# Packed 16-bit keys, shared write-back and a longer taper of loads in a NaN-ignoring row maximum

## The chip, the cores and the metric

The kernel runs on one core of one Trainium2 chip. The metric is the device time in microseconds (us) of one execution; a second number, the span, is the profiled time from the first to the last instruction and is about 1.8 us shorter. PE is not used. In the profile ACT is ScalarE, POOL is GpSimd, DVE is VectorE and SPq is the queue that issues the transfers.

## The reference

The input is 32 x 2048 rows of 2048 float32 values, a tenth of them NaN. The output is one maximum per row, NaNs ignored:

```python
def reference(x, axis):
    return np.nanmax(x, axis=axis).astype(np.float32)
```

That is 65,536 rows of 8 KB, 537 MB, read once. Rows are spread over 128 partitions, 512 for each partition. Below, "a row" is one row of every partition: 2048 elements in each partition, 1 MB in all.

## The kernel before

A tile of up to 8 rows is loaded. ScalarE maps the upper 16 bits of every float, as an integer, to a key that puts NaN at the bottom; GpSimd maps the key back; VectorE then takes the float maximum. Both passes touch every second 16-bit element *in place*, in the loaded tile. A last pair of small VectorE operations (`none`, `fin`) marks rows without a number, and a small store follows.

```python
FULL = [[3, 3, 2]]                       # one load of 8 rows, worked on in pieces of 3, 3, 2
GROUPS = [[FULL] * 5] * 12 + [           # 12 groups of five tiles, then four groups of one
    [FULL],
    [[[2, 2], [2], [2]]],                # loads of 4, 2, 2
    [[[2], [2], [1], [1], [1], [1]]],
    [[[1], [1], [1], [1], [1], [1], [1], [1]]],
]
WIDE = 8
# ... cut ...
io = ctx.enter_context(tc.tile_pool(name="io", bufs=3))      # three tiles of 64 KB a partition
for s, g in zip(rows, GROUPS):
    # ... cut ...
    for tl in g:
        xt = io.tile([P, WIDE * D], i32, tag="xt")
        base = at
        for ld in tl:
            c = sum(ld)
            nc.sync.dma_start(out=xt[...], in_=xg[...])               # L86
            if len(stores) > 1:
                nc.sync.dma_start(**stores.pop(0))                    # L91, same queue
            for c in ld:
                xp = xt[:, (at - base) * D : (at - base + c) * D]
                nc.scalar.activation(                                 # L94
                    out=xp.bitcast(u16)[:, 1::2], in_=xp.bitcast(i16)[:, 1::2],
                    func=PRELU, bias=top, scale=-1.0, alpha=...)
                nc.gpsimd.tensor_scalar(                              # L102
                    out=xp.bitcast(i16)[:, 1::2], in0=xp.bitcast(u16)[:, 1::2],
                    scalar1=-1.0, scalar2=float(TOP), op0=ALU.mult, op1=ALU.add)
                nc.vector.tensor_reduce(out=acc[:, at : at + c], ...) # L110
                at += c
    none = res.tile([P, s], i32, tag="none")
    nc.vector.tensor_scalar(out=none, in0=acc, ...)                   # L118
    fin = res.tile([P, s], i32, tag="fin")
    nc.vector.tensor_tensor(out=fin, in0=acc.bitcast(i32), in1=none, ...)  # L127
    stores.append(dict(out=og, in_=fin))
```

## Time and profile before

| | before |
|---|---|
| time, median | 1284.1 us |
| span | 1282.3 us |
| last input packet ends | 1268.0 us |
| busy: ScalarE, GpSimd, VectorE | 1203, 1204, 1143 us |

Throughput of the input over the run, in 40 equal slices of 32 us (from the page of the profile):

```profile
GB/s 425 425 425 446 438 425 426 442 440 428 425 438 442 429 425 432 448 429 426 429 448 432 425 429 446 433 423 428 448 430 430 427 448 428 431 427 433 304 245 197
```

The input flows at some 433 GB/s until the last three slices, where it drops to 304, 245 and 197. The same in stretches, with how busy each engine was (columns: stretch, its length, busy us and instructions of DVE, ACT and POOL, a clock of no use here, DMA share, GB/s):

```profile
30.00:1180.00 1150.00, 1044.72 (x199) 1112.41 (x178) 1114.15 (x178) 1.00 1.00 433
1180.00:1200.00 20.00, 18.68 (x4) 19.41 (x5) 19.42 (x4) 1.00 0.62 266
1200.00:1220.00 20.00, 19.54 (x6) 20.00 (x5) 19.68 (x5) 1.00 0.92 381
1220.00:1240.00 20.00, 20.00 (x7) 16.32 (x5) 19.68 (x5) 1.00 0.47 187
1240.00:1260.00 20.00, 20.00 (x9) 15.19 (x7) 16.87 (x8) 1.00 0.78 318
1260.00:1285.00 25.00, 19.73 (x12) 11.08 (x5) 13.49 (x6) 1.00 0.32 132
```

Until 1180 us the DMA share is 1.00: the transfers bound the kernel, and ScalarE and GpSimd are just able to follow. Afterwards the DMA has holes, but VectorE and GpSimd are nearly gapless (from 1200 us on, VectorE's longest gap is 0.43 us and GpSimd's 2.65). What each piece of work costs, from the groups by shape (busy us and mean ns of one stand after the bar):

```profile
L94 ACT ACTIVATE xt<-xt,top 128x4096 uint16<-128x4096 int16 x67 | 323.3, 4839 | 0.0
L102 POOL TENSOR_SCALAR xt<-xt 128x4096 int16<-128x4096 uint16 x67 | 318.0, 4746 | 5.3
...
L94 ACT ACTIVATE xt<-xt,top 128x2048 uint16<-128x2048 int16 x12 | 30.0, 2566 | 8.5 <-DMA xt<-in_x_dram 8.5
...
L118 DVE TENSOR_SCALAR none<-acc 128x40 int32<-128x40 f32 x12 | 16.4, 1363 | 0.4
L118 DVE TENSOR_SCALAR none<-acc 128x8 int32<-128x8 f32 x4 | 8.1, 2014 | 0.0
```

Two rows cost ScalarE 4.84 us and one row 2.57, so a further row costs 2.27 us. The DMA brings a row in 2.42. `none`, on 8 to 40 elements, takes 1.4 to 2 us, which can't be work. VectorE's order of time at the end (start, duration):

```profile
1222.33 4.10 DVE L118 TENSOR_SCALAR none<-acc 128x8 int32<-128x8 f32 x1
1226.27 4.41 DVE L110 TENSOR_REDUCE acc<-xt 128x2 f32<-128x4096 f32 x1
1230.60 0.56 DVE L127 TENSOR_TENSOR fin<-acc,none 128x8 int32<-128x8 int32 x1
1231.09 13.06 DVE L110 TENSOR_REDUCE acc<-xt 128x2 f32<-128x4096 f32 x3
1244.07 1.88 DVE L118 TENSOR_SCALAR none<-acc 128x8 int32<-128x8 f32 x1
...
1266.15 13.24 DVE L110 TENSOR_REDUCE acc<-xt 128x1 f32<-128x2048 f32 x6
1279.42 0.17 DVE L118 TENSOR_SCALAR none<-acc 128x8 int32<-128x8 f32 x1
```

The last `none`, when GpSimd has finished, takes 0.17 us; the ones before it, 1.88 to 4.10. In the trace every one of the fifteen before the last ended 0.02 to 0.04 us after the end of a GpSimd instruction that was already running when it started: it waits for GpSimd.

### The profile page before, as it was taken

Reading aid. Unit: us, or ns where it says so; the run is one execution under the profiler, and the core shown is the slowest. Engines: PE = TensorE matmul, PEld = TensorE weight load, DVE = VectorE, ACT = ScalarE, POOL = GpSimd, SP = SyncE. Lnnn points to the kernel's source line nnn. Section 1 sums busy time; section 2 is a strip of 40 time slices with the busy share of each in tenths; the row PEclk is TensorE's granted clock in tenths of the full one; section 3 lists DMA queues with packets and bytes.
Section 4 is the critical chain, followed back from the end, with each engine's and each line's share of the span. In section 5 each row is a group of like instructions: output and inputs, shape, how many; then the busy total and the mean of one; then the engine's idle time right before and its main releaser. Section 6 shows DMA issues by size and latency. Waiting matters only on the chain.

```text
span 1282.3 us, 1065 instructions
## 1 busy us (share of the span) xinstructions
DVE 1142.7 (89%) x234; ACT 1203.3 (94%) x203; POOL 1203.8 (94%) x205
## 2 busy tenths in 40 slices
DVE  0789989989998998998998998998998998998999
ACT  3999999999999999999999999999999999999985
POOL 0999999999999999999999999999999999999996
DMA  9999999999999999999999999999999999999754
GB/s 425 425 425 446 438 425 426 442 440 428 425 438 442 429 425 432 448 429 426 429 448 432 425 429 446 433 423 428 448 430 430 427 448 428 431 427 433 304 245 197
DMA packets 13543, 537.20 MB, mean 419 GB/s; under 512 B 3552, under 2 KB 3552, under 8 KB 3552
## 3 DMA queue, kind: packets, MB, share of 16 engines
q1 hardware_dynamic: 13536, 537.14, 97.1%
q14 instruction: 7, 0.06, 0.0%
HBM read 536.87 MB, written 0.26 MB: 419 GB/s over the span
## 4 chain that ended last, share of the span: by engine, by line
DMA 42%; POOL 23%; DVE 18%; ACT 12%; issue 5%; ACTq 0%; DVEq 0%
DMA xt<-in_x_dram 42%; POOL xt L102 23%; DVE acc L110 18%; ACT xt L94 12%; DVE none L118 1%; DVE fin L127 0%; ACTq L94 0%; DVEq L110 0%; DVEq L127 0%
## 5 line engine op out<-in xcount | busy, mean ns | idle before, releaser
L102 POOL TENSOR_SCALAR xt<-xt 128x6144 int16<-128x6144 uint16 (+2 forms) x201 | 1203.6, 5988 | 69.9 <-ACT xt L94 58.9
L94 ACT ACTIVATE xt<-xt,top 128x6144 uint16<-128x6144 int16 (+2 forms) x201 | 1201.8, 6082 | 67.0 <-DMA xt<-in_x_dram 67.0
L110 DVE TENSOR_REDUCE acc<-xt 128x3 f32<-128x6144 f32 (+2 forms) x201 | 1116.0, 5582 | 135.4 <-POOL xt L102 135.4
L118 DVE TENSOR_SCALAR none<-acc 128x40 int32<-128x40 f32 (+1 forms) x16 | 24.4, 1526 | 0.5
L127 DVE TENSOR_TENSOR fin<-acc,none 128x40 int32<-128x40 int32 (+1 forms) x16 | 4.4, 275 | 0.4
L71 ACT ACT_TABLE_LOAD x1 | 1.3, 1283 | 0.7 <-PEq L149 0.7
L69 DVE MEMSET top<- 128x1 f32 x1 | 0.1, 59 | 0.8 <-PEq L149 0.8
L149 POOL MEMSET const-float32-0.0<- 128x1 f32 x1 | 0.1, 98 | 0.2 <-issue 0.2
L71 ACT ACTIVATE warm<-top 128x1 f32<-128x1 f32 x1 | 0.2, 203 | 0.0
L149 POOL MEMSET const-bfloat16-1.0<- 128x1 bf16 x1 | 0.1, 102 | 0.0
L149 POOL MEMSET const-uint8-127<- 128x1 uint8 x1 | 0.1, 102 | 0.0
L149 POOL MEMSET const-float32-1.0<- 128x1 f32 x1 | 0.1, 98 | 0.0
## 6 DMA issues: line engine op xcount, KB each, us to landing
xt<-in_x_dram SPq DMA_DIRECT2D x12, 1024.0 KB, 9.7
xt<-in_x_dram SPq DMA_DIRECT2D x4, 2048.0 KB, 13.9
xt<-in_x_dram SPq DMA_DIRECT2D x1, 4096.0 KB, 16.1
xt<-in_x_dram SPq DMA_DIRECT2D x61, 25.8
out_dram<-fin SPq DMA_DIRECT2D x12, 20.0 KB, 25.5
out_dram<-fin SPq DMA_DIRECT2D x4, 4.0 KB, 1.4
```

What stands on the lines that cost most here:

```text
L69: nc.vector.memset(top, EDGE)
L71: nc.scalar.activation(out=warm, in_=top, func=PRELU, alpha=0.5)
L94: nc.scalar.activation(out=xp.bitcast(u16)[:, 1::2], in_=xp.bitcast(i16)[:, 1::2], func=PRELU, bias=top, scale=-1.0, alpha=float(TOP - LOW ...
L102: nc.gpsimd.tensor_scalar(out=xp.bitcast(i16)[:, 1::2], in0=xp.bitcast(u16)[:, 1::2], scalar1=-1.0, scalar2=float(TOP), op0=ALU.mult, op1= ...
L110: nc.vector.tensor_reduce(out=acc[:, at : at + c], in_=xp.bitcast(f32).rearrange("p (c d) -> p c d", c=c), axis=mybir.AxisListType.X, op=A ...
L118: nc.vector.tensor_scalar(out=none, in0=acc, scalar1=NONE, scalar2=float(0x00C00000), op0=ALU.is_equal, op1=ALU.mult,)
L127: nc.vector.tensor_tensor(out=fin, in0=acc.bitcast(i32), in1=none, op=ALU.bitwise_or)
L149: nc = _bacc.Bacc("TRN2", target_bir_lowering=False, num_devices=1)
```

## The change

The intent: ScalarE writes its keys packed into small buffers, which should be faster than every second element in place. The time won on ScalarE is spent on writing back one row of seven (negative numbers in the lists), which relieves GpSimd. With some slack on all three engines a long taper of loads and pieces at the end can bring their lag behind the DMA down. Loads have 7 rows, so that three tiles of 56 KB and the key buffers fit. `none` moves to PSUM, and a group is now six tiles, so fewer results come near the end.

```diff
-FULL = [[3, 3, 2]]
-GROUPS = [[FULL] * 5] * 12 + [ ... cut ... ]
-WIDE = 8
+TILES = (                                    # (loads, pieces, reduces)
+    [([1], [1], [1])]
+    + [([7], [1, 2, 2, -1, 1], [1, 2, 2, 2])] * 59
+    + [([7], [2, 2, 1, 2], [4, 1, 2])]
+    + [([7], [1, 2, 2, -2], [3, 2, 2])]
+    ... cut: two more of one load, then [2, 5] and [4, 3] ...
+    + [([4, 3], [2, 2, 2, -1], [2, 2, 3])] * 3
+    + [([1, 3, 3], [1, 1, 1, 1, 2, -1], [1, 2, 1, 3])]
+    + [([3, 2, 2], [1, 1, 1, 1, 1, 1, 1], [2, 1, 1, 1, 1, 1])]
+    + [([2, 1, 2, 1, 1], [1, 1, -1, 1, 1, 1, 1], [3, 2, 1, 1])]
+    + [([1, 1, 1, 1, 1, 1, 1], [1, 1, -1, 1, 1, 1, 1], [3, 1, 1, 1, 1])]
+    + [([1, 1, 1, 1, 1, 1, 1], [1, 1, -1, 1, 1, 1, -1], [1, 2, 1, 1, 1, 1])]
+)
+GROUPS = [TILES[:7]] + [TILES[i : i + 6] for i in range(7, 73, 6)] + [TILES[73:]]
+WIDE = 7
+PIECE = 2
@@
+    mid = ctx.enter_context(tc.tile_pool(name="mid", bufs=4))
+    flag = ctx.enter_context(
+        tc.tile_pool(name="flag", bufs=2, space=bass.MemoryType.PSUM)
+    )
@@ ... cut: loads of a tile first, then one store if due ...
+            for c in pieces:
+                back, c = c < 0, abs(c)
+                xp = xt[:, at * D : (at + c) * D]
+                kt = mid.tile([P, PIECE * D], u16, tag="kt")
+                nc.scalar.activation(                             # L116
+                    out=kt[:, : c * D],
+                    in_=xp.bitcast(i16)[:, 1::2],
+                    func=ACT.Prelu, bias=top, scale=-1.0, alpha=...)
+                if back:
                     nc.scalar.activation(                         # L125
-                        out=xp.bitcast(u16)[:, 1::2],
-                        in_=xp.bitcast(i16)[:, 1::2],
-                        func=PRELU, ...
+                        out=xp.bitcast(i16)[:, 1::2],
+                        in_=kt[:, : c * D],
+                        func=ACT.Copy, bias=float(TOP), scale=-1.0)
+                else:
                     nc.gpsimd.tensor_scalar(                      # L133
                         out=xp.bitcast(i16)[:, 1::2],
-                        in0=xp.bitcast(u16)[:, 1::2],
+                        in0=kt[:, : c * D], ...)
+                at += c
+                while reds and done + reds[0] <= at:
+                    ... cut: tensor_reduce of the next reds[0] rows, L144 ...
-        none = res.tile([P, s], i32, tag="none")
+        none = flag.tile([P, s], i32, tag="none")
```

## The prediction

> **What bounds the kernel now.** From 30 to 1180 us the input DMA bounds it: the windows view gives a DMA share of 1.00 and 433 GB/s, and each 8-row tile starts on ScalarE 19.36 us after the last, having waited about 0.6 us for DMA. But ScalarE, GpSimd and VectorE are at 1112, 1114 and 1045 us busy of those 1150, so none can catch up. At the end the DMA falls to 266, 280, 315 and 348 GB/s from 1180 us on. The queue's timeline shows why: loads wait for VectorE to free a buffer, and result stores stand in the same queue ahead of them. From 1186 us on compute bounds: 32 rows need 94 us from their first activation to the last reduce. At 433 GB/s the whole input needs 1239 us; the span is 1282.
>
> **Costs read from the trace (groups by form).** Per row (from the differences of 1, 2 and 3 rows): ScalarE 2.27 us, GpSimd 2.28, VectorE's reduce 2.14, DMA 2.42; fixed 0.1 to 0.3 us each. The small "none" operation takes 1.4 to 4.1 us while GpSimd runs but 0.17 us at the end when it does not; the Trainium skill ("SBUF — State Buffer", Who interferes with whom) names a port pair that VectorE's two-port modes and GpSimd lock against each other, which agrees.
>
> **What the change does.**
> 1. ScalarE reads the strided keys and writes them packed. The Trainium skill ("ScalarE: Activation LUTs", What ACT_TABLE_LOAD costs) states about 280 ns + 0.833 ns per element; this trace shows 294 + 1.109. I take the strided 16-bit write in place to be what costs the difference, so a packed write should run near 0.84: 1.7 us a row.
> 2. Of 7 rows GpSimd writes back 6 and ScalarE 1, both strided, at about 2.28 a row. Per 7-row tile (DMA 16.94 us), estimated: ScalarE 7 x 1.71 + 2.27 + fixed = 15.6, GpSimd 14.6, VectorE 15.4. Each gets 1.3 us or more of slack per tile.
> 3. "none" goes to PSUM: 12 x 1.2 us off VectorE.
> 4. The end: loads of 7, 4, 3, 2 and finally 1 row over 14 tiles, and stores that no longer block loads. VectorE's lag (28 us) shrinks by 1.3 us a tile, to about 11.
>
> The steady stage stays DMA-bound. All gain is in the last 100 us.
>
> **Sum.** Start 3.2 us, 512 rows at 2.42 = 1239, about 2 for small packets (8 KB packets took 309 ns, 64 KB 2420): last landing near 1244. Then ScalarE twice, reduce, finish: VectorE ends near 1254.5, plus 2.5 for the store and end (as now) = 1257 span, and 1.7 from span to time, as now: **1258 us, 2.0% less, 8 in 10 between 1251 and 1267.** Chances: faster by over 2% 0.52, within 2% 0.40, slower 0.08.
>
> **What would show it.** ScalarE's two-row packed pass at 3.6 to 3.8 us (4.84 now); its one-row write-back at 2.3 to 2.5; GpSimd 4.7 to 4.8 for two rows; "none" below 0.3 us; DMA share near 1.00 until about 1240; the last reduce ending 9 to 12 us after the last landing.
>
> **What would make it wrong.** If the slow ScalarE rate comes from the strided read, ScalarE needs 19.4 us a tile of 16.9 and the time is about 1430. If GpSimd also speeds up on packed input, VectorE gets its data earlier and 2 us come off. If ScalarE's rate is only 0.88 to 0.9, or VectorE has gaps in the taper, 2 to 8 us come on.

## The result, and the profile after

| | before | after |
|---|---|---|
| time, median | 1284.11 us | 1262.16 us |
| ratio, 95% interval | | 0.9829 (0.9812 to 0.9846) |
| span | 1282.3 us | 1260.4 us |
| last input packet ends | 1268.0 us | 1247.8 us |
| busy: ScalarE, GpSimd, VectorE | 1203, 1204, 1143 us | 1124, 1063, 1127 us |

Ratios here are the mean time of one kernel's fast runs over that of the other's of the same rounds, so not quite the ratio of the medians. The gain is 22 us, 1.7%: a clear gain, but under the 2% line.

Throughput of the changed kernel in 40 slices:

```profile
GB/s 412 437 437 437 435 433 417 434 437 437 436 435 435 427 424 437 436 435 437 435 434 424 426 437 435 437 437 433 435 416 437 437 436 437 417 433 430 425 422 211
```

The same stretches as before:

```profile
30.00:1180.00 1150.00, 1046.69 (x288) 1042.67 (x401) 989.50 (x271) 1.00 1.00 433
1180.00:1200.00 20.00, 20.00 (x6) 19.54 (x10) 18.46 (x7) 1.00 1.00 425
1200.00:1220.00 20.00, 17.88 (x7) 19.58 (x10) 19.36 (x9) 1.00 1.01 420
1220.00:1240.00 20.00, 19.93 (x8) 17.73 (x9) 19.03 (x9) 1.00 1.01 420
1240.00:1260.00 20.00, 17.96 (x11) 12.91 (x7) 9.67 (x4) 1.00 0.24 97
```

In the first 1150 us nothing changed for the time: 433 GB/s and a DMA share of 1.00 in both kernels. ScalarE lost 70 us of work there and GpSimd 125, and that time is idle. The whole gain is at the end, where the DMA now stays full until it has nothing more to bring (e6 below shows that a full DMA alone is not the gain). The idle time of ScalarE before each steady tile shows the slack. Here is a tile of 8 rows before and one of 7 rows after (start, duration, the first passes of the tile together; in brackets the idle time before it and what ended it):

```profile
332.93 18.77 ACT L94 ACTIVATE xt<-xt,top 128x6144 uint16<-128x6144 int16 x3 [0.64 <-DMA xt<-in_x_dram]
497.99 12.99 ACT L116 ACTIVATE kt<-xt,top 128x2048 uint16<-128x2048 int16 x5 [1.58 <-DMA xt<-in_x_dram]
```

ScalarE's slack went from 0.6 to 1.6 us a tile and GpSimd's from about 0.5 to 2.5. VectorE had 1.9 us in a tile of 8 rows and has 1.6 in one of 7, no more than before for a row. The groups that answer to those of before:

```profile
L133 POOL TENSOR_SCALAR xt<-kt 128x4096 int16<-128x4096 uint16 x142 | 676.9, 4767 | 79.5 <-ACT kt L116 73.3
L116 ACT ACTIVATE kt<-xt,top 128x4096 uint16<-128x4096 int16 x144 | 525.2, 3694 | 8.5 <-DMA xt<-in_x_dram 8.5
L116 ACT ACTIVATE kt<-xt,top 128x2048 uint16<-128x2048 int16 x224 | 438.2, 1991 | 119.9 <-DMA xt<-in_x_dram 119.9
...
L125 ACT ACTIVATE xt<-kt 128x2048 int16<-128x2048 uint16 x68 | 168.3, 2475 | 0.2
...
L155 DVE TENSOR_SCALAR none<-acc 128x42 int32<-128x42 f32 x11 | 2.3, 205 | 0.4
```

ScalarE's two-row pass went from 4.84 to 3.69 us, GpSimd's hardly changed (4.75 and 4.77), and `none` is down to 0.2 us. A row more costs ScalarE 3.694 - 1.991 = 1.70 us when it writes packed. VectorE's order of time at the end:

```profile
1211.27 30.66 DVE L144 TENSOR_REDUCE acc<-xt 128x3 f32<-128x6144 f32 x9 [2.12 <-POOL xt L133]
1241.96 0.20 DVE L155 TENSOR_SCALAR none<-acc 128x42 int32<-128x42 f32 x1
1242.20 0.20 DVE L164 TENSOR_TENSOR fin<-acc,none 128x42 int32<-128x42 int32 x1
1242.32 15.38 DVE L144 TENSOR_REDUCE acc<-xt 128x1 f32<-128x2048 f32 x6
1257.73 0.17 DVE L155 TENSOR_SCALAR none<-acc 128x7 int32<-128x7 f32 x1
```

VectorE has no gap from 1211 us on and its last reduce ends at 1257.7 us, 9.9 us after the last packet. Before, 11.4 us lay between (1268.0 and 1279.4), but there the last packet itself was late.

### The profile page after: what moved, and what is told of

Its sections match the earlier page's. It is cut to its first block, busy times and chain, and to the rows that moved or that the text cites. A ratio compares the mean times of both kernels' runs of the same rounds, so it can differ in the third digit from the quotient of the medians.

```text
span 1260.4 us, 1707 instructions
## 1 busy us (share of the span) xinstructions
DVE 1127.1 (89%) x319; ACT 1123.5 (89%) x440; POOL 1063.1 (84%) x302
## 4 chain that ended last, share of the span: by engine, by line
DMA 52%; POOL 15%; ACT 13%; DVE 10%; issue 9%; SPq 0%; ACTq 0%; DVEq 0%
DMA xt<-in_x_dram 52%; POOL xt L133 15%; ACT kt L116 12%; DVE acc L144 10%; ACT xt L125 1%; SPq L103 0%; DVE none L155 0%; ACTq L116 0%; DVEq L144 0%; DVE fin L164 0%; ACTq L125 0%
## 5 line engine op out<-in xcount | busy, mean ns | idle before, releaser
L144 DVE TENSOR_REDUCE acc<-xt 128x2 f32<-128x4096 f32 (+2 forms) x292 | 1122.9, 3889 | 129.3 <-POOL xt L133 129.2
L133 POOL TENSOR_SCALAR xt<-kt 128x2048 int16<-128x2048 uint16 (+1 forms) x298 | 1062.9, 3567 | 189.1 <-ACT kt L116 175.7
L116 ACT ACTIVATE kt<-xt,top 128x2048 uint16<-128x2048 int16 (+1 forms) x368 | 951.1, 2657 | 128.4 <-DMA xt<-in_x_dram 128.4
L125 ACT ACTIVATE xt<-kt 128x2048 int16<-128x2048 uint16 x70 | 177.8, 2540 | 0.3
L155 DVE TENSOR_SCALAR none<-acc 128x42 int32<-128x42 f32 (+2 forms) x13 | 2.6, 202 | 0.5
L164 DVE TENSOR_TENSOR fin<-acc,none 128x42 int32<-128x42 int32 (+2 forms) x13 | 2.6, 197 | 0.4
```

What stands on the lines that cost most here:

```text
L116: nc.scalar.activation(out=kt[:, : c * D], in_=xp.bitcast(i16)[:, 1::2], func=ACT.Prelu, bias=top, scale=-1.0, alpha=float(TOP - LOW) / (E ...
L125: nc.scalar.activation(out=xp.bitcast(i16)[:, 1::2], in_=kt[:, : c * D], func=ACT.Copy, bias=float(TOP), scale=-1.0,)
L133: nc.gpsimd.tensor_scalar(out=xp.bitcast(i16)[:, 1::2], in0=kt[:, : c * D], scalar1=-1.0, scalar2=float(TOP), op0=ALU.mult, op1=ALU.add,)
L144: nc.vector.tensor_reduce(out=acc[:, base + done : base + done + n], in_=xt[:, done * D : (done + n) * D] .bitcast(f32) .rearrange("p (c d ...
L155: nc.vector.tensor_scalar(out=none, in0=acc, scalar1=NONE, scalar2=float(0x00C00000), op0=ALU.is_equal, op1=ALU.mult,)
```

## The experiments

My theory: the 22 us come from two things that need each other, slack on the engines (packed keys and shared write-back) and a long taper that uses the slack to make up lag. Rivals: the taper alone; the small things alone (`none` blocked by GpSimd, stores in the load queue); the split of loads alone. Estimates in the expectations come from a recurrence worked by hand from the trace: each piece starts when its data, its engine and its buffer are there, with the durations above.

### The changed kernel with one part undone

**e1: no split loads.**

```diff
+TILES = TILES[:1] + [([7], pieces, reds) for _, pieces, reds in TILES[1:]]
```

> The changed kernel with every load of the taper made one 7-row load; pieces and reduces stay. My theory (the taper lets the engines start on part of a tile, at a small price in DMA time): the last landing comes 2 to 4 us earlier than 1247.8 us (no small packets), but VectorE ends about 10 us later; time 1270 to 1275 (estimate 1272.7). Rival (the split of the loads is worth nothing, the slack of the engines is all): 1258 to 1263, earlier by the saved packets.

Measured: 1274.5 us, ratio to before 0.9925. The last packet ended at 1246.0 us, 1.8 us earlier than in the changed kernel (expected 2 to 4, so a little less), and VectorE's last reduce at about 1269.9, 12 us later. Splitting the loads is worth 12 us and costs 2 us of transfer; the rival falls.

**e2: GpSimd writes back everything.**

```diff
+TILES = [(loads, [abs(c) for c in pieces], reds) for loads, pieces, reds in TILES]
```

> The changed kernel with GpSimd writing back all pieces, none on ScalarE. My theory (GpSimd at 2.29 us a row plus 0.23 a piece needs 17.2 us for a 7-row tile that the DMA brings in 17.0, so it falls behind and no lag is ever made up): 1280 to 1292 (estimate 1287), no better than before, GpSimd gapless. Rival (the taper alone gives the gain): 1262 to 1266.

Measured: 1299.7 us, ratio 1.012: slower than the kernel before, and beyond my range. The direction is the theory's, the size is not. Its first stretch shows why (columns as above):

```profile
30.00:1180.00 1150.00, 1024.71 (x282) 872.02 (x329) 1124.17 (x327) 1.00 1.00 426
```

GpSimd, at 98% of that stretch, holds the DMA down to 426 GB/s. The last packet ended at 1266.4 us, 19 us later than in the changed kernel, and VectorE's last reduce another 29 us later instead of 10. So of the 37 us about half are the slowed steady stage and half are lag never made up. The estimate missed because my rates (2.29 us a row, 0.227 a piece) gave GpSimd 1256 us for its 512 rows and 368 pieces, and it needed about 1270 without its waits: 0.04 us too little for each piece.

**e3: `none` back in SBUF.**

```diff
-        none = flag.tile([P, s], i32, tag="none")
+        none = res.tile([P, s], i32, tag="none")
```

> The changed kernel with the small none tile back in SBUF. My theory (none then waits for GpSimd's instruction, about 1.2 us each; only the ones near the end lie on the path): +1 to +2 us (1263 to 1264.5), none's mean back over 1 us. Rival (the blocked VectorE was most of what the old ending lost): +6 us or more.

Measured: 1262.9 us, ratio 0.9835 (the changed kernel: 0.9829), so about +0.7 us, a little under the +1 to +2 that I expected. (The intervals of the two ratios overlap, but the slowest run of the changed kernel, 1262.26 us, is below the fastest of this one, 1262.81.) The operation itself became worse than before:

```profile
L155 DVE TENSOR_SCALAR none<-acc 128x42 int32<-128x42 f32 x11 | 33.7, 3063 | 0.4
```

3.06 us each, yet nearly all of it fell into idle time: VectorE's waiting for GpSimd in total dropped from 129 to 99 us. From 1100 us on only one of them was blocked, for 1.6 us at 1150 us. (The kernel before took 1284.1 us in the rounds of both.)

**e4: no taper at all.**

```diff
+TILES = TILES[:2] + [TILES[1]] * 72
```

> The changed kernel with all 73 tiles after the first like the steady ones: one 7-row load, pieces 1,2,2,1 by ScalarE,1. My theory: the last landing near 1244.5 us, then one whole tile must pass the engines (about 25 us to VectorE's end): 1271 to 1278 (estimate 1274), so the keys without taper give about 10 of the 22 us. Rival (taper is all): no better than before, 1284 or more.

Measured: 1275.1 us, ratio 0.9929. The time is as estimated; the last packet came at 1246.0 us, 1.5 later than I expected, and the last reduce ended at 1270.6. All parts of the change but the taper, that is packed keys, shared write-back, PSUM tile, 7-row tiles and the order of the stores together, give 9 of the 22 us. e1, which has the small pieces of the taper but not its small loads, is only 0.6 us faster than this run: the small pieces bring next to nothing without the small loads.

**e10: a taper of three tiles only.**

```diff
+TILES = (TILES[:2] + [TILES[1]] * 69
+    + [([2, 2, 2, 1], [2, 2, 2, -1], [2, 2, 2, 1])]
+    + [([2, 2, 1, 1, 1], [2, 2, 1, 1, -1], [2, 2, 1, 1, 1])]
+    + [([1] * 7, [1, 1, 1, -1, 1, 1, -1], [1] * 7)])
```

> The changed kernel with a taper of only the last three tiles (loads 2,2,2,1, then 2,2,1,1,1, then seven of 1 row), all tiles before them like the steady ones. My theory (the engines make up only 1.3 to 1.7 us of lag in a tile, so a short taper can't bring 25 us of lag down): 1268 to 1273 (estimate 1270.7). Rival (small last loads are enough): 1262 to 1265.

Measured: 1271.0 us, ratio 0.9896. Small last loads are not enough: with them the last reduce still ended 18.7 us after the last packet (1265.9 and 1247.2). Lag comes down only as fast as the slack of a tile allows, so the taper has to be long.

### The keys themselves

**e5: key buffers twice as wide, every second element used** (two buffers of the same total size; single look).

```diff
-    kt = mid.tile([P, PIECE * D], u16, tag="kt")            # bufs=4, kt[:, : c * D]
+    kt = mid.tile([P, PIECE * 2 * D], u16, tag="kt")        # bufs=2, kt[:, 1 : c * 2 * D : 2]
```

> The changed kernel with the key buffers twice as wide and every second 16-bit element used (two buffers for four), so ScalarE writes strided but not in place. If the strided write is what costs: ScalarE's two-row pass goes from 3.69 to about 4.84 us, a tile then needs 19.3 us of ScalarE, and the time is 1400 to 1460. If writing in place was what cost: 3.7 us a pass and 1262 to 1266. GpSimd's two-row pass (4.77 with a packed source) tells whether the source's stride matters to it: 4.75 if not.

Measured: 1477.4 us (one run, state unknown). The groups:

```profile
L116 ACT ACTIVATE kt<-xt,top 128x4096 uint16<-128x4096 int16 x144 | 686.7, 4838 | 17.8 <-POOL xt L133 17.8
L133 POOL TENSOR_SCALAR xt<-kt 128x4096 int16<-128x4096 uint16 x142 | 674.3, 4749 | 176.0 <-ACT kt L116 170.0
...
L125 ACT ACTIVATE xt<-kt 128x2048 int16<-128x2048 uint16 x68 | 168.2, 2474 | 2.2
```

The pass takes 4.838 us although nothing is done in place: the same as in place (4.839). So it is the strided 16-bit *write* that costs. In the changed kernel the read is strided and the pass takes 3.694, and ScalarE's write-back reads packed, writes strided and pays again (2.475 us for one row against 1.991). In this run the write-back also reads strided and takes the same (2.474), so the stride of the read costs ScalarE nothing. GpSimd is the same from a packed or a strided source (4.77 and 4.75 us). The time missed my range by 17 us at the top; ScalarE also waited 29.5 us in all for GpSimd to free one of the only two buffers, which I had left out.

### The kernel before with one part done

**e6: the last stores after all loads.**

```diff
-                if len(stores) > 1:
+                if len(stores) > 1 and gi < 12:             # gi: number of the group; res bufs=6
```

> The kernel before, with the result stores of its last groups after all loads instead of between them (six result buffers for three). My theory (its ending is bound by the three engines, not by the loads: VectorE is gapless from 1200 us on, ScalarE's waits for DMA there are not on the path): 0 to -1.5 us. Rival (the stores that block the queue starve the ending): -5 us or more.

Measured: 1284.3 us, ratio 1.000 (0.998 to 1.002). The stretches of its end:

```profile
1200.00:1220.00 20.00, 19.52 (x6) 20.00 (x6) 19.68 (x5) 1.00 1.00 422
1220.00:1240.00 20.00, 20.00 (x6) 20.00 (x7) 19.68 (x5) 1.00 1.02 423
1240.00:1260.00 20.00, 20.00 (x10) 20.00 (x10) 19.36 (x9) 1.00 0.16 61
1260.00:1285.00 25.00, 20.07 (x13) 1.77 (x1) 11.38 (x5) 1.00 0.01 1
```

The holes in the DMA are gone and the last packet ends at 1244.6 us instead of 1268.0, 23 us earlier, and the time does not move. GpSimd ended 2.2 us earlier too (1271.7 against 1273.9), and only VectorE, without a gap of note from 1200 us on, ended where it did before. So the drop of GB/s at the old kernel's end cost no time by itself, since VectorE was full behind it.

**e7: only `none` in PSUM.**

```diff
-        none = res.tile([P, s], i32, tag="none")
+        none = flag.tile([P, s], i32, tag="none")
```

> The kernel before, with only the small none tile moved to PSUM. My theory: VectorE loses the 1.9 to 4.1 us that none and its neighbour cost in each of the last groups, and then follows GpSimd, which ended at 1273.9 us: -3 to -5 us. Rival (nothing, the lag is GpSimd's and ScalarE's alone): 0 to -1; rival (it is most of the 22 us): -10 or more.

Measured: 1278.5 us, ratio 0.9955: 5.8 us of gain, more than expected, from one small tile. VectorE then ends a reduce behind GpSimd's last piece, as expected, and its last pieces have small gaps:

```profile
1269.38 2.29 DVE L113 TENSOR_REDUCE acc<-xt 128x1 f32<-128x2048 f32 x1 [0.25 <-POOL xt L105]
1271.92 2.29 DVE L113 TENSOR_REDUCE acc<-xt 128x1 f32<-128x2048 f32 x1 [0.25 <-POOL xt L105]
1274.24 0.17 DVE L121 TENSOR_SCALAR none<-acc 128x8 int32<-128x8 f32 x1
```

It follows GpSimd piece by piece, waiting 0.25 us for each. GpSimd had also come forward by 2 us: the last loads were issued 5 us earlier (1246.3 against 1251.4), and its gap of 2.65 us is gone. That part I had counted only in the next run.

**e9: both of these.**

```diff
+ the edits of e6 and e7 together
```

> The kernel before with both small changes, none in PSUM and the last stores after all loads. My theory: GpSimd also loses its 2.7 us gap near the end: -5 to -7 us, and no more, since ScalarE and GpSimd at 19.1 and 18.8 us for what the DMA brings in 19.4 can't make up their lag. Rival (these two small things are the gain): -15 or more.

Measured: 1278.6 us, ratio 0.9955: no more than e7 alone. The last packet ended at 1244.8 us, about 3 us *before* that of the changed kernel, and the kernel is still 16 us slower than it. With so little slack the engines make up hardly any lag: VectorE's last reduce ends 29.3 us after the last packet.

**e8: new loads and long taper, keys in place.**

```diff
+FULL = ([7], [3, 2, 2], [3, 2, 2])
+TILES = [FULL if i in range(1, 60) else (loads, [abs(c) for c in pieces], reds)
+         for i, (loads, pieces, reds) in enumerate(TILES)]
-                    out=kt[:, : c * D],
+                    out=xp.bitcast(u16)[:, 1::2],           # no kt; GpSimd reads it there
```

> The changed kernel's loads, taper, store order and PSUM tile, but the keys in place as before: no packed buffers, all pieces written back by GpSimd, steady tiles in pieces of 3, 2, 2. My theory (a taper without slack makes up little lag): 1276 to 1288 (estimate 1280). Rival (the taper and the small changes are the gain, packing none): 1262 to 1266.

Measured: 1281.7 us, ratio 0.998. The long taper, with PSUM tile and store order, is worth 2.7 us without slack, less than the PSUM tile gave alone; the rival "taper and small things" falls. Its stretches show ScalarE with none left:

```profile
1200.00:1220.00 20.00, 17.73 (x7) 20.00 (x10) 19.45 (x8) 1.00 1.01 423
1220.00:1240.00 20.00, 16.39 (x5) 20.00 (x9) 19.37 (x9) 1.00 1.01 422
```

Four kernels, all with `none` in PSUM and no store in the way, put it together (times in us; the in-place ones also differ in the size of a tile where they have the old loads):

| | short taper | long taper |
|---|---|---|
| keys in place, GpSimd writes all | 1278.6 (e9) | 1281.7 (e8) |
| keys packed, write-back shared | 1271.0 (e10) | 1262.2 (changed kernel) |

With keys in place the long taper costs 3 us, probably since its many small pieces bring fixed costs to full engines (GpSimd's passes sum to 1211 us in e8 and 1203 in e9); the last packet also came 3.4 us later (1248.2 and 1244.8). With packed keys it gains 9. The second row of the table has two parts, and neither alone is enough with these small steady pieces: packed keys with GpSimd writing all took 1299.7 us (e2), shared write-back with strided keys 1477.4 (e5). Not tried were packed keys with GpSimd writing all in larger pieces, the 7-row tile alone, and the old order of the stores in the changed kernel.

### Trying to go further

**e11: the last seven tiles as one group.**

```diff
-GROUPS = [TILES[:7]] + [TILES[i : i + 6] for i in range(7, 73, 6)] + [TILES[73:]]
+GROUPS = [TILES[:7]] + [TILES[i : i + 6] for i in range(7, 67, 6)] + [TILES[67:]]
```

> The changed kernel with the last seven tiles as one group of results, so the second but last none and fin (0.45 us on VectorE at 1242 us) go. VectorE is gapless from 1211 us to its end, so if it bounds the ending: -0.3 to -0.5 us against 1262.16. If the landings bound it: 0.

Measured: 1262.1 us, ratio 0.9826, that is -0.1 us by medians and -0.4 by ratios, whose intervals are wider than that. Inconclusive: at best a few tenths.

**e12: the last 16 tiles searched anew.**

```diff
+TILES = TILES[:58] + [ ... 16 tiles, e.g. ([3, 3, 1], [1, 1, 1, 2, 1, -1], [1, 2, 1, 3]) ... ]
+ the edit of e11
```

> One last group as in the run before, and the pieces, loads and reduces of the last 16 tiles searched anew with a hand recurrence that uses the durations of the changed kernel's trace: estimate -1.1 us against 1262.16, range -2 to +1, since the taper as it stands is close to the best of this form.

Measured: 1263.3 us, ratio 0.9835: 1.2 us slower, outside my range. VectorE was gapless from 1188.8 us on and its last reduce still ended 0.8 us later than that of the changed kernel (1258.5 and 1257.7). It seems to have come into the ending with more work left than my recurrence had given; that was not followed up. The recurrence was right to 0.3 us for e10, to 1 us for e4 and to 2 us for e1 and e8 (13 for e2), so differences of 1 us between tapers are below what it can rank. No version clearly beats the changed kernel.

## Why the prediction was right or wrong

The forecast of 1258 us against 1262.2 was right in its mechanism and inside its range. The most likely class (faster by over 2%) was not the one that came; the line lay at 1258.4.

1. **The DMA bounds the steady stage before and after: right.** 433 GB/s at share 1.00 in both. The gain is all at the end.
2. **The strided write is what slows ScalarE: right, and now shown (e5).** 3.69 us for two rows, predicted 3.6 to 3.8. The fixed and per-element cost, 0.29 us + 0.83 ns, agrees with what the Trainium skill ("ScalarE: Activation LUTs", What ACT_TABLE_LOAD costs) states, about 0.28 us + 0.833 ns, for the packed write only. Write-back 2.475 and GpSimd 4.767 fell inside their ranges too.
3. **"At the end the DMA falls ... The queue's timeline shows why: loads wait for VectorE to free a buffer, and result stores stand in the same queue ahead of them": true as a description, wrong as a cause of lost time.** With the stores out of the way (e6) the last packet came 23 us earlier and the time stayed. "From 1186 us on compute bounds", in the same paragraph, was the right half. Point 4 had no ground to list the stores as a gain; in the changed kernel their order was not tried alone.
4. **`none` in PSUM: seen, but not sized.** I wrote "12 x 1.2 us off VectorE" and gave it no place in the sum. In the old kernel it is worth 5.8 us alone (e7), since three of them stood blocked on a full engine in the last 60 us. In the new one it is worth 0.7 (e3), since VectorE has idle time for most of the run and only one blocked `none` is left after 1100 us. Such worths do not add up: they depend on what else is full.
5. **The lag shrinks through the taper: right, but the number partly by luck.** The last reduce ended 9.9 us after the last packet, predicted 9 to 12. That this needs both slack and length is shown by e4, e8 and e10. But I had let a lag of 28 us shrink by 1.3 us a tile. Without a taper the lag of these engines was 24.6 us (e4), and the fourteen tiles took 14.7 off, about 1.05 each: two errors that cancel.
6. **The term that was mis-sized is the last landing: "near 1244", measured 1247.8 (end of the last packet).** The sum was 3.2 + 1239 + 2. From the records of the packets: the first starts at 1.75 us, where I had 3.2 (-1.4). A row in 56 KB packets costs 2.424 us (e4: 1241.2 us of packet time on each of the 16 DMA engines for 512 rows), not 2.42 (+2.2). Small packets add 2.4 us (1243.6 against 1241.2), not 2 (+0.4). And between first and last packet there are 2.4 us in which an average engine had none, most of it after 1240 us, when the 16 engines run dry one after another (+2.4). Together +3.6. VectorE's end and the span move with it. Another 0.7 us was lost in adding up: 1257 and 1.7 are 1258.7, and I wrote 1258. What makes the engines run dry at different times is not settled: 14 of the 8064 large packets took 0.3 to 0.7 us longer than the usual 2.12, which would do it if a few engines had most of them; the records do not tell the engines apart.

## What to carry to other kernels

When a transfer bounds the steady stage, faster engines gain nothing there; they gain the ability to make up lag before the end, and that takes both slack per tile and a taper long enough to spend it (here ScalarE and VectorE had 1.6 us a tile in the steady stage; fourteen tiles brought the lag from 24.6 us to 9.9, three only to 18.7). A hole in the DMA at the end is no proof that loads are late: ask first whether an engine behind it is full, and close the hole alone to see. A tiny operation with a duration that can't be its work is waiting inside its own record, and what that costs depends on whether its engine is full at that moment.

## What the Trainium skill lacked or had wrong

- "SBUF — State Buffer" (Door 1, the note on cachelines) says 16-bit data can be strided by up to 8 elements for free. For reads by ScalarE that holds (stride 2: 0.83 ns per element). For writes it does not: 16-bit writes at stride 2 took 1.11 ns per element on ScalarE, in place (4.839 us for 4096 elements) and not in place (4.838), against 0.83 packed.
- "ScalarE: Activation LUTs" (What ACT_TABLE_LOAD costs) gives 0.833 ns per element for every function without this exception.
- "GPSIMD Engine Reference" (3.1, Elementwise) gives 1.03 cycles per element for bodies of one or two operations, 0.86 ns at the 1.2 GHz it uses, and does not say for which layout of the operands. A two-operation `tensor_scalar` with a strided 16-bit output took (4.767 - 2.475) us / 2048 = 1.12 ns here, from a packed and from a strided source. Whether a packed output makes it faster was not tried.
- "SBUF — State Buffer" (Who interferes with whom) is right that VectorE can be locked out by GpSimd, and these runs give a size: a 42-element operation with SBUF output took 3.06 us on average and up to 4.39, next to GpSimd instructions of up to 4.77, and 0.205 with its output in PSUM. Every long one ended 0.04 us after the GpSimd instruction beside it. Only the size is new.
- "DMA: Bandwidth & Descriptors" (Specifications) lists about 358 GB/s, half of what a stack gives, as the HBM limit of a core. That did not bind here: this one-core kernel read HBM at 433 GB/s for 1150 us, next to the 435 that the page gives for the fabric. A later section of the page (Measured) agrees, with 425 GB/s for one core alone, so only the row of the table misleads. The page has no figure for how unevenly the 16 engines end a long stream (here about 2.4 us).
